# A hybrid attention block on one NeuronCore: seven-product keys and values in the stick-breaking units alone, the mask moved into the scan, the softmax scaling on VectorE, and the input's sums tied to their places

## The chip, the core and the metric

The kernel runs on one core of one Trainium2 chip. A core has a matrix engine (TensorE, in the profile PE, with its weight loads as PEld), a vector engine (VectorE, DVE), an engine for activation functions (ScalarE, ACT), a general engine (GpSimd, POOL) and a sync engine that issues DMAs (SyncE, SP). Each runs its own instructions in a fixed order; semaphores tie them together. Matrix results land in PSUM, everything else lives in SBUF. DMAs are issued from the queues of SP and ACT, and from GpSimd where the transfer has to add to what is already in its destination.

The metric is device time in microseconds of one execution, lower is better. The profiled execution is one execution out of several, and its trace lists each instruction with its start, its length and the source line that made it.

## The reference

One decoder block over 16 meta tokens and 512 tokens, 1024 wide, all in float32. Every token is normalized and projected to ten pieces. Eight heads do differential attention with ALiBi, sixteen heads of 64 do stick-breaking attention, both are gated with SiLU, projected, merged by sigmoid gates, projected once more and normalized over the residual. Cut to what matters here:

```python
proj = jnp.einsum('bld,dn->bln', h, w_in[i])
q_d, k_d, v_d, g_d, q_s, k_s, v_s, g_s, m_d, m_s = jnp.split(proj, IN_OFFSETS, axis=-1)

# differential attention, per head: two softmaxes, their difference weighs the values
s = einsum(q, k) * 64 ** -0.5 + alibi          # -inf where the key lies behind the query
p = softmax(s)
y_d = einsum(p[:, :, 0] - lam * p[:, :, 1], v)

# stick-breaking attention, per head; before: k_pos < q_pos
z = einsum(q, k) * 64 ** -0.5
log_keep = where(before, log_sigmoid(-z), 0)
suffix = cumsum_from_the_right(log_keep) - log_keep
a = where(before, exp(log_sigmoid(z) + suffix), 0)
y_s = einsum(a, v)

br_d = einsum(rms_norm(y_d) * (1 - lam_init) * silu(g_d), w_br_diff)
br_s = einsum(y_s * silu(g_s), w_br_sb)
y = einsum(sigmoid(m_d + b0) * br_d + sigmoid(m_s + b1) * br_s, w_out)
out = layer_norm(DN_ALPHA * h + y)
```

The queries come in five blocks: the 16 meta tokens, whose results are dropped, and four blocks of 128. A query block sees 144, 272, 400 or 528 keys.

## The kernel before

**Precision by three products.** [...] Each product of 128 x 128 weights with a piece of the input is three matmuls: high by high, high by low, low by high. A weight half (128 x 512) is loaded by SP (`fetch`, L134), rounded by ScalarE (`hi`, L160) and its remainder taken by VectorE (`lo`, L165). `prep` does this for one half, four halves ahead of use, and then lets `fetch` load what the rings of buffers have room for. `take` checks that the halves are used in the order of the list `seq`, from which `items` (what is split) and `loads` (what is loaded) are made ahead of time.

**Units.** The attention runs in 16 units: eight heads of differential attention (d0 to d7), then eight pairs of stick-breaking heads (s0 to s7). The loop at the end of the attention section runs, for unit u, a list of projections (keys and values of unit u + 1, the query of unit u + 2, and in the stick-breaking units two gate projections) and, woven into it at given points of a rough clock, the steps of unit u's own attention: scores, transposes, values. `run` walks the projections, adds up the time they are taken to need and drops each step in when its point has come.

**Keys and values by seven products.** `keys_values` picks one of two ways. In the plain way `stage_k` and `stage_v` (both through `proj_pos`, matmuls at L475) project each of the two 264-position halves of the input with all eight weight tiles: 2 x 2 x 8 x 3 = 96 matmuls of 264 columns. From unit number `SEVEN` on, `stage_kv` does it with seven block products in the manner of Strassen and Winograd: 7 x 4 x 3 = 84 matmuls (L626). That needs sums of weight blocks and of input blocks. Of the weights, with (a11, a12) and (a21, a22) for keys and values, the list has a21 - a11 and a21 + a22, made by a load of a21 and a second load that adds a11 or a22 to it (`accum_op=ALU.add` at L136, issued by GpSimd into the ring `rawk`), and two more sums that VectorE makes (`add`, L147). `stage_kv` also copies and combines its partial results (L637 to L646) on the way to the keys (L633) and to `vT`, the values before their transpose.

**The input's sums.** For the seven products the input halves are combined too: `input_sums(k)`, for k from 0 to 3, copies the meta columns (GpSimd, L597), makes four sums on VectorE (L599 to L602), rounds them on ScalarE (L604) and takes the remainder (L605). The results are `tS` and the list `tL`. The condition on u in the unit loop puts two of these calls into each of the two units ahead of the unit that first projects with them.

**Who orders the work.** In the start of the kernel and in everything behind the attention, `keep_order` ties each instruction to the one before it on its engine, as the program lists them. In the units there is no such tie, apart from a few that `behind` makes on ScalarE: there a planner simulates the program, as it is being built, and orders each engine's queue by when it thinks that the instructions can run. So the place in the program's text and the place in an engine's queue differ. `follow` adds a tie without a semaphore between two instructions.

**Differential attention** (`d_scores`). For each of four query blocks and two softmaxes: scores on PE (L692), bias and minimum on VectorE (L775), exponential with its sum on ScalarE (L779). Then VectorE takes reciprocals (L783), GpSimd scales the first softmax (L784, up to 128 x 528) and makes the small factor of the second (L785), and VectorE combines them into the weights (L786). The weights are transposed on PE (L698, L703), split (L708, L709) and multiplied with the values (`d_values`, to L803); squares and the norm follow (`d_norm`).

**Stick-breaking attention** (`s_scores`). Two sigmoids on ScalarE (L840 of minus z, L842 of z) give the shares kept and taken. GpSimd zeroes the taken shares in the diagonal block where the key is not before the query (L846). VectorE scans the kept shares from the right (L848): the state is multiplied by the kept share and then the greater of it and a mask `after` is taken; the mask is 1 where the key is not before the query, so that the state starts at 1 there. The product of taken share and scanned neighbour (L849) is the weight.

**Other names.** `ident` is the 128 x 128 identity. `L` is 528, `H2` 264, `P` 128, `NB` 4. `gate` multiplies a gate with an attention result on GpSimd (L491). `vT` has one buffer; so has each of the two tiles `e0`, `e1` for exponentials or sigmoids. `pj` is a ring of three PSUM banks for all projections.

Of the kernel before, what the change touches and what calls it, by code (L numbers as in the profile page):

```python
# [9 lines left out]
F32 = mybir.dt.float32  # L10
# [3 lines left out]
ALU = mybir.AluOpType  # L14
PSUM = bass.MemoryType.PSUM

P = 128
# [4 lines left out]
L = M + S  # L22
# [12 lines left out]

ORDERED = [mybir.EngineType.PE, mybir.EngineType.DVE, mybir.EngineType.Activation, mybir.EngineType.Pool]
WARM = 14
SEVEN = 4
TD = (0.85, 11.0, 14.5)
QOFF = [0, 96, 224, 352, 480]  # L40
LO, HI = slice(0, 64), slice(64, 128)
# [3 lines left out]
def hybrid_block_kernel(ctx: ExitStack, tc: tile.TileContext, x, meta, emb_g, emb_b, w_in, b_gate,  # L45
                        diff_lambda, subln_g, w_br_d, w_br_s, w_out, ln_g, ln_b, out):
    nc = tc.nc
    v, s, g, pe = nc.vector, nc.scalar, nc.gpsimd, nc.tensor
# [22 lines left out]
    for u, (kind, n) in enumerate(UNITS):  # L71
        if u + 1 < len(UNITS):
            other, i = UNITS[u + 1]
# [39 lines left out]
    for l in range(WOUT, len(loads)):  # L113
        left[l] = 1
    raw0 = ypool.tile([P, 4, KT, P], F32, tag="ys", name="raw0")
    raws, split, sums, later = {}, [], {}, []
    rings = {"raw": (6, []), "rawk": (4, []), "rawa": (4, [])}
    state = {"l": 0, "h": 0, "n": 0, "ahead": 4}
    pools = {"raw": wpool}
# [5 lines left out]
    def fetch(most=99):  # L125

        while state["l"] < len(loads) and most:
            l = state["l"]
            src, more, tag = loads[l]
            bufs, log = rings[tag]  # L130
            if len(log) >= bufs and left[log[-bufs]] or tag not in pools:
                return
            raw = pools[tag].tile([P, 4, P], F32, tag=tag, name=tag, bufs=bufs)
            nc.sync.dma_start(raw if l < WOUT else raw.rearrange("p a b -> p (a b)"), src)  # L134
            if more is not None:
                g.dma_start(raw, more, accum_op=ALU.add)  # L136
            raws[l] = raw
            log.append(l)
            state["l"] += 1
            most -= 1  # L140

    def add(h):

        first, second = items[h]
        one = sums.pop(True) if first is None else raws[first]
        raw = one if first is None else pools["sum"].tile([P, 4, P], F32, tag="sum", name="sum", bufs=1)
        v.tensor_tensor(raw, one, raws[second], op=ALU.add)  # L147
        for l in items[h]:
            if l is not None:
                left[l] -= 1  # L150
        sums[h] = sums[True] = raw

    def hi(h):

        assert len(split) == h
        item = items[h]
        raw = raw0[:, h // 2, ts(h % 2, 4)] if item is None else sums.pop(h) if isinstance(item, tuple) else raws[item]
        wh, wl = [wpool.tile([P, 4, P], F32R, tag=w, name=w, bufs=6) for w in ("wh", "wl")]
        split.append((raw, wh, wl))
        s.copy(wh, raw)  # L160
# [26 lines left out]
    def follow(ins, other):  # L187
        tc.add_manual_dep(ins, other.name, mybir.DependencyInfo(mybir.DependencyClass.NoSync, mybir.DependencyReason.DATA),
                          reason="order")

    def behind(name, on=True):

        if on:
            ins = nc.cur_bb.bb.instructions[-1]
            if name in state:
                follow(ins, state[name])
            state[name] = ins

    def keep_order(first, engines=ORDERED):

# [318 lines left out]
    with tc.tile_pool(name="att", bufs=1) as ap:  # L519
# [14 lines left out]
        for t in (v4d, v4s, *(tails[n][1] for n in tails)):  # L534
            g.memset(t.bitcast(F32), 0.0)
        E = [ap.tile([P, ZW], F32, name=f"e{c}") for c in range(2)]
        after, staged = [], []


        K = [ap.tile([P, 2, L], F32R, name=f"k{c}") for c in range(2)]  # L540
# [53 lines left out]
        def input_sums(k):  # L594


            g.tensor_copy(hP[k][:, :, :M], hM[:, k:k + 5:4])  # L597
            b11, b12, b21, b22 = [hP[k][:, m, ts(n, H2)] for m in range(2) for n in range(2)]
            v.tensor_tensor(b22, b12, b22, op=ALU.subtract)  # L599
            v.tensor_tensor(b12, b11, b12, op=ALU.subtract)  # L600
            v.tensor_tensor(b11, b22, b11, op=ALU.subtract)
            v.tensor_tensor(b21, b11, b21, op=ALU.add)  # L602
            h, l = tS[0][:, k:k + 5:4], pair_of("tl", F32R)
            s.copy(h, hP[k])  # L604
            v.tensor_tensor(l, hP[k], h.bitcast(F32), op=ALU.subtract)  # L605
            tL.append(l)
# [143 lines left out]
        def d_scores(unit, h):  # L750

            A = unit["A"]


            bias = ap.tile([P, L], F32, tag="bias", name="bias", bufs=2)
            if h == 0:
                g.iota(bias, pattern=[[-1, L]], base=400, channel_multiplier=1, allow_small_or_imprecise_dtypes=True)
                g.affine_select(bias, bias, pattern=[[-1, L]], compare_op=ALU.is_ge, fill=1e30, base=400,
                                channel_multiplier=1)
            g.tensor_scalar(bias, biases[-1] if h else bias, 0.5 if h else -0.5, None, op0=ALU.mult)  # L760
            biases.append(bias)
            a = apads[h % 2]
            mn = ap.tile([P, NB, 2, 2], F32, tag="mn", name="mn", bufs=2)
            zs = ap.tile([P, NB, 2], F32, tag="zs", name="zs", bufs=2)
            rz = ap.tile([P, NB, 2], F32, tag="rz", name="rz", bufs=2)
            for i in reversed(range(NB)):
                nk = NKEY[i]
                e = [E[c][:, ZOFF[i]:ZOFF[i] + nk] for c in range(2)]
                for c in range(2):
                    m = mn[:, i, c, :]  # L770
                    for n, (ps, k0, use) in enumerate(logits(A[c], K[c], i)):
                        if n == 1:
                            yield
# [9 lines left out]
                v.reciprocal(r, zs[:, i, :])  # L783
                g.tensor_scalar(e[0], e[0], r[:, 0:1], None, op0=ALU.mult)  # L784
                g.tensor_tensor(r[:, 1:2], r[:, 1:2], nlam, op=ALU.mult)  # L785
                v.scalar_tensor_tensor(a[:, AOFF[i]:AOFF[i] + nk], e[1], r[:, 1:2], e[0], op0=ALU.mult, op1=ALU.add)  # L786
                yield

# [41 lines left out]
        def s_scores(unit, c, first):  # L830
            A = unit["A"]
            a = apads[c]
            sg, om = E
            for i in reversed(range(NB)):
                nk, z0 = NKEY[i], ZOFF[i]
                for n, (ps, k0, use) in enumerate(logits(A[c], K[c], i)):
                    if n == 1:
                        yield
                    o = ds(z0 + k0, use)
                    s.activation(om[:, o], ps[:, :use], AF.Sigmoid, scale=-1.0)  # L840
                    behind("act", first)
                    s.activation(sg[:, o], ps[:, :use], AF.Sigmoid)  # L842
                    behind("act", first)

                own = sg[:, ds(z0 + nk - P, P)]
                g.affine_select(own, own, pattern=[[-1, P]], compare_op=ALU.is_gt, fill=0.0, base=0, channel_multiplier=1)  # L846
                rev = om[:, z0:z0 + nk][:, ::-1]
                v.tensor_tensor_scan(rev, rev, after[0][:, L - nk:][:, ::-1], 1.0, ALU.mult, ALU.max)  # L848
                v.tensor_tensor(a[:, ds(AOFF[i], nk - 1)], sg[:, ds(z0, nk - 1)], om[:, ds(z0 + 1, nk - 1)],  # L849
                                op=ALU.mult)  # L850
                yield
# [36 lines left out]
        for u, (kind, n) in enumerate(UNITS):  # L888
# [9 lines left out]
            if u + 4 in (SEVEN + 1, SEVEN + 2):  # L898
                if not tS:
                    tS.append(ypool.tile([P, KT, L], F32R, tag="ys", name="tS"))  # L900
                for m in range(2):
                    steps.append((5.0 + 6.0 * m, lambda k=2 * (u + 3 - SEVEN) + m: input_sums(k)))
            if kind == "d":
                ta = {}
                steps += spread(d_scores(unit, n), 0.0, TD[0], 10)
# [3 lines left out]
                pending = [(3.0 if n < 7 else 5.8, lambda unit=unit, n=n: d_norm(unit, n))]  # L909
            else:  # L910
                if n == 0:
                    after.append(ap.tile([P, L], F32, tag="bias", name="after", bufs=2))
                    g.memset(after[0], 0.0)
                    own = after[0][:, L - P:]
                    g.affine_select(own, own, pattern=[[-1, P]], compare_op=ALU.is_gt, fill=1.0, base=0, channel_multiplier=1)
                    for a in apads:
                        for i in range(NB):
                            g.memset(a[:, ds(AOFF[i] + NKEY[i] - 1, 1)], 0.0)
# [259 lines left out]
```

## Time and profile before

| what | value |
|---|---|
| median of three runs | 742.61 us |
| lowest and highest of the three | 742.55 and 744.74 us |
| the profiled execution's own time | 746.39 us |
| its span, from the first to the last instruction | 744.7 us |
| mean granted clock of TensorE | 0.983 |
| DMA over the span | 105.02 MB, 141 GB/s |
| GpSimd's DMA queue | 12.06 MB, 12.8% of 16 engines' span |

How to read it: the page gives for each engine its busy time, then groups of instructions with count, busy time, mean length and the idle time just ahead of them with the instruction that ended it. Matmuls are pipelined and each is drawn longer than the distance to the next one, so a busy PE does not by itself mean that nothing can be gained; the distance from start to start tells what a matmul takes, and PE's waits and the granted clock tell what is lost. The chain of waits follows the work that ended last back through whoever released it. An engine's idle time counts only where this chain runs through it.

The units can be told apart in the trace by the query projections, each of which ends with ScalarE rounding the query (L551): between two of these lie one unit's projections. The start lies ahead of 37 us, the units with differential heads reach to about 250 us, the stick-breaking ones to about 545 us, and the projections behind them to the end.

### The profile page before, as it was taken

To read this page: it belongs to the slowest core of one execution; us is meant where nothing else is said; L and a number is where in the kernel's file an instruction comes from. 1 tells how busy PE (TensorE), PEld (TensorE's weight loads), DVE (VectorE), ACT (ScalarE), POOL (GpSimd) and SP (SyncE) were. 2 spreads that over 40 slices of the span, in tenths; PEclk is the share of its full clock that TensorE was granted. 3 is DMA by queue.
4 is the path that set the end of the run, shared out by engine and by line. 5 is a ranking of instruction groups with operands and counts; after the bars stand their busy time and mean duration, and the time that the engine had idled before them with its cause. 6 is when DMAs were issued, how large, how long until landed. Compare 5 with 4: busy or idle time off the path is not lost.

```text
span 744.7 us, 13453 instructions
## 1 busy us (share of the span) xinstructions
PE 716.7 (96%) x4546; PEld 651.2 (87%) x4546; DVE 597.4 (80%) x1214; ACT 441.2 (59%) x1043; POOL 212.3 (29%) x269
## 2 busy tenths in 40 slices
PE   8899999998999898999999999999999999999995
PEld 8799999987988787888989898988888998899885
DVE  6986678887888767979797989878566778688897
ACT  5675667676667966656656565656544555656300
POOL 3343453453463313232323121214002201240002
PEclk9989999999999998999999999999999999999998
DMA  9374444647555544455655524395229747787802
GB/s 291 89 153 119 133 98 114 162 104 164 141 113 130 136 128 108 135 123 144 140 158 117 140 90 126 104 304 147 71 83 184 157 100 180 147 169 186 320 27 105
DMA packets 160135, 105.02 MB, mean 141 GB/s; under 512 B 7441, under 2 KB 148146, under 8 KB 160066
## 3 DMA queue, kind: packets, MB, share of 16 engines
q1 hardware_dynamic: 137762, 91.04, 41.5%
q0 software_dynamic: 21984, 12.06, 12.8%
q10 hardware_dynamic: 320, 1.06, 0.4%
q8 instruction: 36, 0.59, 0.3%
q14 instruction: 33, 0.27, 0.1%
HBM read 82.53 MB, written 7.86 MB: 121 GB/s over the span
## 4 chain that ended last, share of the span: by engine, by line
PE 80%; DVE 7%; DMA 4%; POOL 3%; issue 3%; ACT 3%; SPq 0%; ACTq 0%; DVEq 0%; POOLq 0%
PE q L626 15%; PE ps L460 11%; PE ps L459 11%; PE ps L461 11%; PE q L985 9%; PE ps L475 6%; PE sc L692 5%; PE t L698 3%; DMA lgb<-in_ln_b_dram 1%; PE t L703 1%; DMA rawk<-in_w_in_dram 1%; PE bank L350 1%; PE av L862 1%; PE av L863 1%; POOL e L784 1%
## 5 line engine op out<-in xcount | busy, mean ns | idle before, releaser
L165 DVE TENSOR_TENSOR wl<-raw,wh 128x512 fp32r<-128x512 f32 x168 | 121.2, 726 | 41.7 <-ACT wh L160 40.2
L460 PE MATMUL ps<-hTl,wh 128*128 128x512 f32 x368 | 146.7, 399 | 0.0
L459 PE MATMUL ps<-hTh,wh 128*128 128x512 f32 x368 | 145.8, 396 | 0.0
L461 PE MATMUL ps<-hTh,wl 128*128 128x512 f32 x368 | 145.3, 395 | 0.0
L160 ACT CAST wh<-raw 128x512 fp32r<-128x512 f32 x168 | 102.9, 621 | 35.5 <-PE ps L460 20.6
L461 PEld LDWEIGHTS ps<-hTh,wl 128*128 128x128 f32 x368 | 69.6, 189 | 12.9
L459 PEld LDWEIGHTS ps<-hTh,wh 128*128 128x128 f32 x368 | 69.6, 189 | 12.8
L460 PEld LDWEIGHTS ps<-hTl,wh 128*128 128x128 f32 x368 | 69.6, 189 | 12.1
L692 PE MATMUL sc<-k,A 128*128 128x264 f32 (+3 forms) x320 | 66.7, 301 | 4.1 <-ACT e L842 2.3
L846 POOL TENSOR_SCALAR_AFFINE_SELECT e<-e 128x128 f32<-128x128 f32 x64 | 43.6, 702 | 93.0 <-ACT e L842 84.5
L985 PE MATMUL q<-gh,wl 128*128 128x256 f32 x224 | 63.9, 285 | 0.0
L985 PE MATMUL q<-gl,wh 128*128 128x256 f32 x224 | 63.7, 284 | 0.0
L985 PE MATMUL q<-gh,wh 128*128 128x256 f32 x224 | 63.2, 282 | 0.2 <-ACT t L994 0.2
L784 POOL TENSOR_SCALAR e<-e,rz 128x528 f32<-128x528 f32 (+3 forms) x32 | 46.1, 1441 | 56.9 <-DVE rz L783 56.9
L136 POOL DMA_DIRECT2D rawk<-in_w_in_dram x24 | 32.4, 1381 | 99.5 <-DMA rawk<-in_w_in_dram 62.2
L709 DVE TENSOR_TENSOR al<-t,ah 128x512 fp32r<-128x512 f32 (+2 forms) x88 | 45.7, 525 | 18.4 <-ACT ah L708 11.2
L692 PEld LDWEIGHTS sc<-k,A 128*128 128x128 f32 x320 | 51.4, 192 | 9.2 <-ACT e L842 2.7
L848 DVE TENSOR_TENSOR_SCAN e<-e,after 128x528 f32<-128x528 f32 (+1 forms) x64 | 55.4, 871 | 4.8 <-ACT e L840 4.6
L708 ACT CAST ah<-t 128x512 fp32r<-128x512 f32 (+2 forms) x88 | 40.1, 464 | 30.0 <-PE t L698 21.9
L626 PE MATMUL q<-tS,wh 128*128 128x264 f32 x192 | 56.0, 292 | 0.8 <-DVE A L552 0.7
L626 PE MATMUL q<-tl,wh 128*128 128x264 f32 x192 | 55.4, 289 | 0.0
L626 PE MATMUL q<-tS,wl 128*128 128x264 f32 x192 | 55.0, 288 | 0.0
(278 smaller groups left out, 1976.7 us busy)
## 6 DMA issues: line engine op xcount, KB each, us to landing
raw<-in_w_in_dram SPq DMA_DIRECT2D x140, 256.0 KB, 3.1
k<-ks SPq DMA_DIRECT2D x60, 132.0 KB, 2.7
rawk<-in_w_in_dram SPq DMA_DIRECT2D x24, 256.0 KB, 3.4
rawk<-in_w_in_dram POOLq DMA_DIRECT2D x24, 256.0 KB, 5.2
raw<-in_w_out_dram SPq DMA_DIRECT2D x16, 256.0 KB, 3.7
k<-ks SPq DMA_DIRECT2D x60, 66.0 KB, 2.2
raw<-in_w_br_diff_dram SPq DMA_DIRECT2D x12, 256.0 KB, 3.4
raw<-in_w_br_sb_dram SPq DMA_DIRECT2D x12, 256.0 KB, 4.2
```

Source lines behind the costliest of these rows:

```text
L160: s.copy(wh, raw)
L165: eng.tensor_tensor(wl, raw, wh.bitcast(F32), op=ALU.subtract)
L459: pe.matmul(ps, wh[:, k % 4, :], hTh[:, k, M:], start=(k == 0), stop=False)
L460: pe.matmul(ps, wh[:, k % 4, :], hTl[:, k, M:], start=False, stop=False)
L461: pe.matmul(ps, wl[:, k % 4, :], hTh[:, k, M:], start=False, stop=(k == KT - 1))
L475: pe.matmul(ps[:, :H2], a[:, k % 4, :], b[:, k, ts(c, H2)], start=(k == 0 and m == 0), stop=(k == KT - 1 and m == 2))
L626: pe.matmul(bank, a[:, k, :], b, start=start and k == 0 and j == 0, stop=k == 3 and j == 2, skip_group_check=not start)
L692: pe.matmul(ps[:, :n], q, K[:, m, k0:k0 + n], start=(m == 0), stop=(m == 1))
L709: v.tensor_tensor(l, t[:, o:o + w], h.bitcast(F32), op=ALU.subtract)
L784: g.tensor_scalar(e[0], e[0], r[:, 0:1], None, op0=ALU.mult)
L848: v.tensor_tensor_scan(rev, rev, after[0][:, L - nk:][:, ::-1], 1.0, ALU.mult, ALU.max)
L985: pe.matmul(bank, a[:, k, :], b[:, n, k, :], start=start and k == 0 and m == 0, stop=k == 3 and m == 2, skip_group_check=not start)
```

## The change

1. `SEVEN` goes from 4 to 8: the units d4 to d7 project keys and values in the plain way, and the seven products begin with s0. The conditions on `SEVEN` follow: the input's sums are now called in the units d5 and d6, and `seq`, `items` and `loads` have plain weight halves for d4 to d7.
2. The accumulating second load is no longer issued in `fetch` right behind the first. It is kept in `second` and issued by `added`: for the ring `rawk` two calls of `prep` later, or at once where an `add` or a `hi` needs it before; for the ring `rawa`, used behind the attention, at once as before.
3. A new helper `placed` runs a piece of the program and ties its first instruction on each named engine behind the last one that the program lists there. The accumulating loads are placed on GpSimd, the input's sums on all four engines.
4. In `d_scores` the scaling and the small factor move from GpSimd to VectorE.
5. In `s_scores` the mask on GpSimd goes. The scan starts from 0 in place of 1, and its second operand is the identity in the last 128 columns: the state is 0 until the query's own key, 1 there, and the running product of kept shares behind it. A weight multiplies a taken share with the scanned neighbour, which is now 0 wherever the key is not before the query.

```diff
-SEVEN = 4
+SEVEN = 8
...
             nc.sync.dma_start(raw if l < WOUT else raw.rearrange("p a b -> p (a b)"), src)
             if more is not None:
-                g.dma_start(raw, more, accum_op=ALU.add)
+                second[l] = lambda raw=raw, more=more: g.dma_start(raw, more, accum_op=ALU.add)
+                later.append((state["n"] + (2 if tag == "rawk" else 0), lambda l=l: added(l)))
+                later.sort(key=lambda x: x[0])
+                if tag == "rawa":
+                    added(l)
...
+    def added(l):
+
+        if l in second:
+            placed(second.pop(l), ORDERED[3:])
+
     def add(h):
 
-        first, second = items[h]
+        first, other = items[h]
+        for l in items[h]:
+            added(l)
...
     def hi(h):
...
         item = items[h]
+        added(item)
...
+    def placed(work, engines=ORDERED):
+
+        ins = nc.cur_bb.bb.instructions
+        n = len(ins)
+        work()
+        for e in engines:
+            new = next((i for i in ins[n:] if i.engine == e), None)
+            old = next((ins[m] for m in range(n - 1, max(n - 400, 0), -1) if ins[m].engine == e), None)
+            if new is not None and old is not None:
+                follow(new, old)
...
                 v.reciprocal(r, zs[:, i, :])
-                g.tensor_scalar(e[0], e[0], r[:, 0:1], None, op0=ALU.mult)
-                g.tensor_tensor(r[:, 1:2], r[:, 1:2], nlam, op=ALU.mult)
+                v.tensor_scalar(r[:, 1:2], r[:, 1:2], nlam, None, op0=ALU.mult)
+                v.tensor_scalar(e[0], e[0], r[:, 0:1], None, op0=ALU.mult)
...
-                own = sg[:, ds(z0 + nk - P, P)]
-                g.affine_select(own, own, pattern=[[-1, P]], compare_op=ALU.is_gt, fill=0.0, base=0, channel_multiplier=1)
                 rev = om[:, z0:z0 + nk][:, ::-1]
-                v.tensor_tensor_scan(rev, rev, after[0][:, L - nk:][:, ::-1], 1.0, ALU.mult, ALU.max)
+                v.tensor_tensor_scan(rev, rev, diag[0][:, L - nk:][:, ::-1], 0.0, ALU.mult, ALU.max)
...
-                    steps.append((5.0 + 6.0 * m, lambda k=2 * (u + 3 - SEVEN) + m: input_sums(k)))
+                    steps.append((5.0 + 6.0 * m, lambda k=2 * (u + 3 - SEVEN) + m: placed(lambda: input_sums(k))))
...
-                    after.append(ap.tile([P, L], F32, tag="bias", name="after", bufs=2))
-                    g.memset(after[0], 0.0)
-                    own = after[0][:, L - P:]
-                    g.affine_select(own, own, pattern=[[-1, P]], compare_op=ALU.is_gt, fill=1.0, base=0, channel_multiplier=1)
+                    diag.append(ap.tile([P, L], F32, tag="bias", name="diag", bufs=2))
+                    g.memset(diag[0], 0.0)
+                    g.tensor_copy(diag[0][:, L - P:], ident)
```

More of the change, by code (lines that the diff above doesn't have):

```diff
@@ L115, in hybrid_block_kernel @@
     raw0 = ypool.tile([P, 4, KT, P], F32, tag="ys", name="raw0")
-    raws, split, sums, later = {}, [], {}, []
+    raws, second, split, sums, later = {}, {}, [], {}, []
     rings = {"raw": (6, []), "rawk": (4, []), "rawa": (4, [])}
@@ L140, in fetch @@
             most -= 1
+    def added(l):
+        if l in second:
+            placed(second.pop(l), ORDERED[3:])
     def add(h):
-        first, second = items[h]
+        first, other = items[h]
+        for l in items[h]:
+            added(l)
         one = sums.pop(True) if first is None else raws[first]
         raw = one if first is None else pools["sum"].tile([P, 4, P], F32, tag="sum", name="sum", bufs=1)
-        v.tensor_tensor(raw, one, raws[second], op=ALU.add)
+        v.tensor_tensor(raw, one, raws[other], op=ALU.add)
         for l in items[h]:
@@ L536, in hybrid_block_kernel @@
         E = [ap.tile([P, ZW], F32, name=f"e{c}") for c in range(2)]
-        after, staged = [], []
+        diag, staged = [], []
         K = [ap.tile([P, 2, L], F32R, name=f"k{c}") for c in range(2)]
```

## The prediction

> **What bounds the kernel now.** I read the page first.
>
> ```profile
> span 744.7 us, 13453 instructions
> PE 716.7 (96%) x4546; PEld 651.2 (87%) x4546; DVE 597.4 (80%) x1214; ACT 441.2 (59%) x1043; POOL 212.3 (29%) x269
> PE 80%; DVE 7%; DMA 4%; POOL 3%; issue 3%; ACT 3%; SPq 0%; ACTq 0%; DVEq 0%; POOLq 0%
> ```
>
> TensorE (PE) carries 80% of the chain that ends last, so time can leave only where PE waits, or runs at a lower clock after a wait. Next I read the waits of PE alone: who waited for whom, us in total, times, longest. These are the ones over 0.5 us behind the first matmuls.
>
> ```profile
> PE q L626 <- DVE vT L646: 6.1, 4, 2.4
> PE av L863 <- DVE al L709: 3.6, 1, 3.6
> PE ps L475 <- ACT k L569: 2.5, 1, 2.5
> PE sc L692 <- ACT e L842: 2.3, 1, 2.3
> PE sc L692 <- POOL k L542: 1.2, 1, 1.2
> PE q L626 <- DVE A L552: 0.7, 1, 0.7
> ```
>
> Then PE by stretches, cut where the clock changes: the stretch, its length, PE's busy time and count, the granted clock, DMA share and GB/s.
>
> ```profile
> 36.46:43.29 6.83, 6.14 (x28) 0.50 1.11 144
> 186.65:190.06 3.41, 3.41 (x18) 0.50 0.09 20
> 254.91:258.33 3.42, 3.42 (x11) 0.50 0.00 0
> 285.63:292.46 6.83, 5.17 (x21) 0.50 0.56 115
> ```
>
> The four longest waits each meet a stretch at half clock, which costs about half its length again: 3.4, 1.7, 1.7 and 3.4 us. In four groups by place: **G1**, the start: 2.5 + 1.2 + 3.4 = 7.1. **G2**, the units d3 to d7, waits for the values' copy vT and for A: 6.1 + 0.7 + 1.7 = 8.5. **G3**, at 253 us, where the scores' PSUM waits for ScalarE: 2.3 + 1.7 = 4.0. **G4**, at 287 us in the first stick-breaking unit s0: 3.6 + 3.4 = 7.0. Together 26.6.
>
> The chain of waits in three of these places shows who is late (start, us, what).
>
> ```profile
> 31.52 0.04 POOLq L525
> 33.40 0.53 POOL k L542
> 35.75 0.90 ACT tS L604
> 36.73 0.38 ACT k L569
> 37.15 1.03 PE ps L475 x3
> ...
> 173.33 4.67 DMA rawk<-in_w_in_dram
> 178.56 1.28 POOL rawk L136
> 179.84 1.66 POOL e L784
> 185.49 0.44 DVE vT L646
> 185.97 1.14 PE q L626 x6
> ...
> 284.82 0.83 POOL e L846
> 287.29 0.50 PE av L863
> ```
>
> First block: the input sums' ScalarE cast (L604), written in units d1 and d2, runs in the start between PE and the first keys. Second: GpSimd's queue sits on the accumulating load, so the softmax scaling behind it (L784) is late, then the copy of the values, then PE. Third: the same in s0 with the mask (L846). In G2 and G4, then, attention is late by a queue, not by a full engine.
>
> **The change part by part.**
>
> **Seven products for four units fewer.** d4 to d7 go from 84 to 96 matmuls of 264 columns.
>
> ```profile
> 440.75 2.70 PE q L626 x22
> L165 DVE TENSOR_TENSOR wl<-raw,wh 128x512 fp32r<-128x512 f32 x168 | 121.2, 726 | 41.7 <-ACT wh L160 40.2
> L599 DVE TENSOR_TENSOR hF<-hF x4: 425/428/430, 29.9 to 31.7; 128x264 f32<-128x264 f32 x4
> 66.40:90.80 24.40, 24.40 (x175) 23.12 (x174) 17.14 (x48) 15.99 (x43) 8.53 (x10) 1.00 0.41 109
> 159.20:183.40 24.20, 23.24 (x161) 21.44 (x159) 19.62 (x50) 15.12 (x39) 10.40 (x11) 1.00 0.71 159
> 183.40:209.80 26.40, 24.00 (x157) 22.56 (x157) 21.27 (x55) 18.15 (x48) 12.05 (x13) 0.94 0.57 131
> 209.80:234.10 24.30, 22.62 (x159) 21.06 (x157) 21.22 (x53) 17.62 (x48) 11.06 (x17) 1.00 0.51 127
> ```
>
> A dense run spaces them 2.70/22 = 0.123 us, so 4 x 12 x 0.123 = **+5.9** on PE, with nothing to hide it. The last four rows are one unit each, cut where a query projection is rounded (busy time and count of PE, PEld, DVE, ACT, POOL, then the clock). The first, with plain products, takes 24.4 us with PE busy throughout. Those with seven have 12 x 0.123 = 1.5 us less for PE, 22.9, and still take 24.2, 26.4 and 24.3. Plain products hardly lengthen these units, because the waits of G2 fill the difference. VectorE loses three splits and two sums per unit, 5 x 0.726, and three half-width evictions of 0.43 (the 264 columns of L599): 4.9 us. ScalarE loses three casts. Twelve loads of 256 KB go, eight of them accumulating, and with these the queue's block in most of G2.
>
> **The scaling from GpSimd to VectorE.** Per head four multiplies and four small products change engine.
>
> ```profile
> L784 POOL TENSOR_SCALAR e<-e,rz 128x528 f32<-128x528 f32 (+3 forms) x32 | 46.1, 1441 | 56.9 <-DVE rz L783 56.9
> L303 DVE TENSOR_SCALAR xn<-xt,xmv,xrs 128x512 f32<-128x512 f32 x7 | 3.5, 532 | 1.7 <-POOL xrs L265 1.7
> 31.23 0.21 DVE L413 TENSOR_SCALAR nlam<-lexp 128x1 f32<-128x1 f32 x1
> DVE apad L786 <- POOL rz L785: 9.4, 10, 2.4
> ```
>
> The nearest row is L303, 532 ns for 512 columns. A head has 528 + 400 + 272 + 144 = 1344, so 1.4 us, and 4 x 0.21 = 0.8 for the small ones: 2.2 of VectorE per head. The upper end is 2.7, at the 726 ns of L165; the lower is below nothing, because VectorE's own waits for GpSimd, 9.4/8 = 1.2 per head, go. I take 2.2, as load. It lies beside PE while VectorE has room: the plain unit's 17.1 of 24.4 becomes 19.3. In the chain of a head a step of 1.4 us on GpSimd becomes one of about 0.4, without a crossing of engines. On the sum this is worth nothing by itself, since PE sets the unit.
>
> **The scan without the mask.** 64 selects leave GpSimd. The scan keeps its size and count (only its start value and second operand differ). The new diagonal, a memset and one copy, I cost at nothing; GpSimd is 29% busy, and without that cover it would be one instruction.
>
> ```profile
> L846 POOL TENSOR_SCALAR_AFFINE_SELECT e<-e 128x128 f32<-128x128 f32 x64 | 43.6, 702 | 93.0 <-ACT e L842 84.5 <-DMA ydT<-gd 2.9 <-DVE apad L849 2.8
> POOL rawk L136 <- DMA rawk<-in_w_in_dram: 62.2, 9, 10.9
> ```
>
> **The accumulating loads put off.** GpSimd waited 62.2 us for the first half of such a tile. Issued two splits later, it finds more of them landed. Behind it in GpSimd's queue then stand the gate products, the bias and the rest of the square, and none of these is in PE's waits above. The sum on VectorE that reads the tile could come late: 0, or one landing as at 173 us, +4.7. I take 0, because loads are fetched several tiles ahead. With the mask gone this is the cure of G4: **-5.0** of 7.0, bounds 0 and -7.0, with 2.0 left for lag that d7 hands on.
>
> **The input sums to their places**, now d5 and d6.
>
> ```profile
> L605 DVE TENSOR_TENSOR tl<-hF,tS x4: 1240/1254/1495, 37.2 to 43.6; 128x1056 fp32r<-128x1056 f32 x4
> 35.70 0.43 DVE L568 TENSOR_TENSOR k<-ps,k 64x264 fp32r<-64x264 f32 x1
> ```
>
> They ran from 30 to 44 us. By L599's row the first two start ahead of nlam (L413), which ends at 31.44; the att buffers lie in the memory that the start gives back then, and GpSimd goes on at 31.52. More of them stand ahead of the key remainder L568, whose chain with ScalarE's L569 releases PE at 37.15. PE's 48 products were done 1.2 us before the memset's end at 33.9, near 32.8. Without the sums nlam ends 0.7 earlier, the memset too, and the key evictions (four to six steps of about 0.4) end near 33.3. G1 shrinks to about 0.5 us. A gap that short should cost no clock: three of the four vT waits, 6.1 - 2.4 = 3.7 together, had no half clock behind them. So **-6.6**, bounds 0 and -7.1.
>
> In d5 and d6 they add 16 x 0.425 + 4 x 1.254 = 11.8 to VectorE, 5.9 a unit: 17.1 + 2.2 + 5.9 = 25.2 against PE's 24.4. This is the weak point. I expect a lag of a few us that PE covers with projections, and a piece of G2 to stay: **-6.0** of 8.5. Bounds: -8.5, and +9.6 (rival A, which takes G3 and G4 with it).
>
> **G3** I leave, **0** (bounds -4.0 and 0): its release is ScalarE's own, at the change from the exponential to the sigmoid, which no edit moves.
>
> On the clock, the trace has a half-speed stretch behind a wait of 2.4 us (186 us). [...]
>
> **Sum.** +5.9 - 6.6 - 6.0 - 5.0 = -11.7. The profiled execution took 746.39 (span 744.7 and 1.7 around it), so another like it would take 734.7. The median of the three runs is 742.61, 3.8 lower, and I forecast that: **730.9**.
>
> **The rivals.**
>
> A, the one that ends slower: VectorE becomes the bound in d5, d6 and d7. For it: 25.2 us of work in 24.4. Price: from 159 to 210 us, where attention lagged, VectorE was busy 40.89 of 50.6 us, a share of 0.81. At that share d5 and d6 take 25.2/0.81 = 31.1, 6.7 over each, and d7 takes (21.2 + 2.2)/0.81 = 28.9 against 22.9 of PE, 6.0 over: 19.4 of waits. The waits of G2 to G4, 12.7, had 6.8 of clock behind them, so about half as much again: 29.1 in place of 19.5. That gives 742.6 + 5.9 - 6.6 + 9.6 = **751.5**. It decides from the point where waits and clock behind 115 us pass 20.2. Against it: the share of 0.81 came with VectorE's waits for GpSimd and with GpSimd's for loads, which leave. 0.13, of it 0.03 where it stops within 0.3% of before.
>
> B, the tie does not do what it says: only the first instruction of each engine is tied, or other early work takes the sums' place. G1 stays: **737.5**. Against it: the later sums read what the first wrote. 0.13.
>
> C, lag from d5 to d7 lands in s0, and G4 stays: **735.9**. For it: the last step there, al L709, is VectorE's own. 0.13.
>
> D, no wait is left at all, G3's too, if PE has projections in hand there: 742.6 + 5.9 - 26.6 = **721.9**. Against it: nothing takes ScalarE's change of function away. 0.13.
>
> **How the numbers follow.** The forecast has 0.48, with 726 to 735 for itself. D reaches down to 721.9, B and C up to 737.5, and the milder part of A to about 740. The range is 721 to 740 and leaves out most of A. About 0.3% (2.2 us) is what a measurement of this kernel can tell from no change. Faster: 0.48 + 3 x 0.13 = 0.87, less 0.02 for B and C together with some of A, 0.85; within 0.3% 0.05; slower 0.10.
>
> **What would show it.** Right: L599 to L605 run in d5 and d6; PE's gap near 33 us is under 1 us, with full clock up to 60 us; d3 to d6 without the sums take some 24.4 us with PE full; GpSimd has no L784 or L846; PE's waits and clock behind 115 us come to 9 or less. VectorE busy over 24 us of a unit in d5 and d6, with PE waiting behind it, shows A. The forecast is wrong where PE waits for tS, tl or vT at d7, where the start's wait stays over 2 us, or where another step of VectorE ends PE's wait in s0.

## The result, and the profile after

| | before | after |
|---|---|---|
| median | 743.67 us (4 runs, 742.55 to 746.83) | 732.33 us (4 runs, 731.37 to 734.11) |
| ratio of the two | | 0.9843, 95% interval 0.9805 to 0.9882 |
| span of the profiled execution | 744.7 us | 732.3 us |
| mean granted clock | 0.983 | 0.993 |

The changed kernel is 11.3 us faster by the medians and 12.4 by the spans; 730.9 was forecast, in a range of 721 to 740. In the listing of the changed kernel the lines are some 23 higher: L626 is now L649, L692 L715, L784 L808, L848 L869. First the page after.

```profile
span 732.3 us, 13316 instructions
PE 713.7 (97%) x4594; PEld 649.9 (89%) x4594; DVE 585.8 (80%) x1246; ACT 428.9 (59%) x1023; POOL 111.9 (15%) x133
```

PE has 48 matmuls more (4594 for 4546), as the four plain units ask, and the span is shorter all the same. GpSimd's busy time is nearly halved. The waits of PE after, those over 0.4 us behind the first matmuls of the kernel and ahead of the last projection:

```profile
PE av L880 <- DVE a L752: 3.0, 1, 3.0
PE t L726 <- DVE al L732: 1.3, 1, 1.3
PE q L649 <- DVE vT L669: 0.5, 1, 0.5
```

All of G1 to G4 is gone from this list. The start first, in the chain of waits after:

```profile
32.72 0.54 POOL k L565
33.31 0.39 PE sc L715
```

PE goes on at 33.3 in place of 34.1 and 37.2, and no half clock follows (1.00 from 33 to 60 us). Then the units (stretch, length, and busy time and count of PE, PEld, DVE, ACT, POOL, then clock, DMA share, GB/s): one plain unit without input sums and the two with them.

```profile
134.10:157.50 23.40, 23.40 (x167) 22.13 (x166) 17.07 (x54) 15.03 (x42) 5.80 (x6) 1.00 0.50 109
157.50:182.70 25.20, 25.20 (x183) 23.92 (x182) 22.65 (x66) 17.88 (x46) 3.39 (x2) 1.00 0.60 143
182.70:207.40 24.70, 24.70 (x178) 23.35 (x177) 23.50 (x67) 18.27 (x45) 3.04 (x3) 1.00 0.34 90
```

PE is busy in every one of them, also where VectorE is busy 23.50 of 24.70 us, 95%. G3 was the change of ScalarE from exponentials to sigmoids. The groups of its table loads, before and then after, without the one at the very start:

```profile
L840 ACT ACT_TABLE_LOAD x3 | 3.8, 1283 | 0.1
L779 ACT ACT_TABLE_LOAD x1 | 1.3, 1283 | 0.0
L821 ACT ACT_TABLE_LOAD x1 | 1.3, 1283 | 0.0
L823 ACT ACT_TABLE_LOAD x1 | 1.3, 1283 | 0.0
L819 ACT ACT_TABLE_LOAD x1 | 1.3, 1283 | 0.0
```

```profile
L863 ACT ACT_TABLE_LOAD x2 | 2.6, 1283 | 0.0
L842 ACT ACT_TABLE_LOAD x1 | 1.3, 1283 | 0.0
```

Before, s0's first sigmoids (L840) stood in ScalarE's queue ahead of d6's norm (L821, L823) and d7's last softmax (L779), so the tables went back and forth: seven loads of 1.28 us, 9.0 in all. L819 (L842 after) is the load ahead of d7's own norm, which falls among s0's sigmoids in both kernels. After there are three loads. So G3 too was attention being late: d6 and d7 were not done when s0 began.

What is new is the wait of 3.0 us near 336 us. The timeline of GpSimd and of VectorE there (start, length; in brackets the idle time before), and then the stretch behind it with its clock:

```profile
323.00 1.30 POOL L514 TENSOR_TENSOR ys<-sg,ys 128x512 f32<-128x512 f32 x1 [11.74 <-DVE ys L888]
324.24 2.60 POOL L136 DMA_DIRECT2D rawk<-in_w_in_dram  x2
334.14 0.69 DVE L158 TENSOR_TENSOR sum<-rawk,raw 128x512 f32<-128x512 f32 x1 [5.12 <-DMA rawk<-in_w_in_dram]
```

```profile
336.33:339.74 3.41, 3.33 (x11) 0.50 0.47 138
```

The two accumulating loads stand on GpSimd behind a gate product that waited 11.74 us for VectorE. They are issued at 324 us, and VectorE's sum (L158) stands still for 5.12 us until they land; behind it in VectorE's queue waits what PE needs. PE runs 3.41 us at 0.50 here. The wait of 1.3 us near 440 us has the same chain:

```profile
429.88 7.91 DMA rawk<-in_w_in_dram
437.82 0.69 DVE sum L158
439.41 0.59 DVE al L732
440.05 0.33 PE t L726
```

### The profile page after: what moved, and what is told of

Same layout as the page of the kernel before. It is cut to its first block, busy times and chain, and to the rows that moved or that the text cites. A ratio compares the mean times of both kernels' runs of the same rounds, so it can differ in the third digit from the quotient of the medians.

```text
span 732.3 us, 13316 instructions
## 1 busy us (share of the span) xinstructions
PE 713.7 (97%) x4594; PEld 649.9 (89%) x4594; DVE 585.8 (80%) x1246; ACT 428.9 (59%) x1023; POOL 111.9 (15%) x133
## 4 chain that ended last, share of the span: by engine, by line
PE 64%; issue 16%; DMA 7%; DVE 7%; POOL 4%; ACT 3%; SPq 0%; POOLq 0%; DVEq 0%; ACTq 0%
PE ps L498 12%; PE ps L484 9%; PE ps L482 9%; PE ps L483 9%; PE q L1005 8%; PE q L649 4%; PE sc L715 4%; PE t L721 2%; DMA raw<-in_w_out_dram 2%; DMA ss<-sm 1%; POOL rawk L136 1%; PE bank L373 1%; DMA rawk<-in_w_in_dram 1%; PE t L726 1%; POOL yd L514 1%
## 5 line engine op out<-in xcount | busy, mean ns | idle before, releaser
L177 DVE TENSOR_TENSOR wl<-raw,wh 128x512 fp32r<-128x512 f32 x172 | 119.2, 698 | 43.1 <-ACT wh L172 42.6
L172 ACT CAST wh<-raw 128x512 fp32r<-128x512 f32 x172 | 105.4, 622 | 40.2 <-PE ps L483 28.9
L484 PEld LDWEIGHTS ps<-hTh,wl 128*128 128x128 f32 x368 | 69.5, 189 | 13.3
L482 PEld LDWEIGHTS ps<-hTh,wh 128*128 128x128 f32 x368 | 69.5, 189 | 13.2 <-DVE kvt L666 0.5
L483 PEld LDWEIGHTS ps<-hTl,wh 128*128 128x128 f32 x368 | 69.4, 189 | 12.6
L498 PE MATMUL ps<-hTh,wh 128*128 128x264 f32 x256 | 73.6, 288 | 0.0
L498 PE MATMUL ps<-hTl,wh 128*128 128x264 f32 x256 | 73.4, 287 | 0.0
L498 PE MATMUL ps<-hTh,wl 128*128 128x264 f32 x256 | 73.3, 287 | 0.0
L715 PE MATMUL sc<-k,A 128*128 128x264 f32 (+3 forms) x320 | 66.2, 297 | 0.2 <-POOL k L565 0.2
L869 DVE TENSOR_TENSOR_SCAN e<-e,diag 128x528 f32<-128x528 f32 (+1 forms) x64 | 55.6, 876 | 3.7 <-ACT e L863 3.3
L715 PEld LDWEIGHTS sc<-k,A 128*128 128x128 f32 x320 | 50.4, 189 | 3.5 <-POOL k L565 0.4
L498 PEld LDWEIGHTS ps<-hTh,wl 128*128 128x128 f32 x256 | 48.3, 189 | 0.5
L498 PEld LDWEIGHTS ps<-hTl,wh 128*128 128x128 f32 x256 | 48.3, 189 | 0.4
L498 PEld LDWEIGHTS ps<-hTh,wh 128*128 128x128 f32 x256 | 48.3, 189 | 0.4
```

The costliest lines, as they stand in the source:

```text
L177: eng.tensor_tensor(wl, raw, wh.bitcast(F32), op=ALU.subtract)
L482: pe.matmul(ps, wh[:, k % 4, :], hTh[:, k, M:], start=(k == 0), stop=False)
L483: pe.matmul(ps, wh[:, k % 4, :], hTl[:, k, M:], start=False, stop=False)
L484: pe.matmul(ps, wl[:, k % 4, :], hTh[:, k, M:], start=False, stop=(k == KT - 1))
L498: pe.matmul(ps[:, :H2], a[:, k % 4, :], b[:, k, ts(c, H2)], start=(k == 0 and m == 0), stop=(k == KT - 1 and m == 2))
L715: pe.matmul(ps[:, :n], q, K[:, m, k0:k0 + n], start=(m == 0), stop=(m == 1))
```

## The experiments

Each kernel is compared with runs of the kernel before on the same chip, whose medians were 745.4, 744.7, 746.0 and 745.5 us in the four groups, so the ratios compare better across groups than the times.

| kernel | median, us | ratio to before (95%) | span, us |
|---|---|---|---|
| the change | 732.33 | 0.9843 (0.9805 to 0.9882) | 732.3 |
| a1, loads early, untied | 729.08 | 0.9781 (0.9755 to 0.9808) | 727.5 |
| a2, SEVEN = 4 | 739.22 | 0.9910 (0.9877 to 0.9942) | 737.4 |
| b1, before + sums tied | 740.05 | 0.9928 (0.9906 to 0.9950) | 741.2 |
| a3, scaling on GpSimd | 740.00 | 0.9918 (0.9893 to 0.9943) | 740.1 |
| a7, a1 + SEVEN = 4 | 732.97 | 0.9849 (0.9830 to 0.9867) | 731.3 |
| a8, a1 + scaling on GpSimd | 730.21 | 0.9813 (0.9797 to 0.9830) | 727.7 |
| a9, a1 + mask on GpSimd | 732.10 | 0.9838 (0.9810 to 0.9865) | 730.8 |
| a5, a1 + sums untied | 731.55 | 0.9831 (0.9813 to 0.9849) | 729.4 |
| a6, loads late, untied | 732.54 | 0.9814 (0.9765 to 0.9863) | 730.7 |
| b2, before + SEVEN = 8 | 732.33 | 0.9815 (0.9790 to 0.9840) | 730.7 |
| c1, a1 + SEVEN = 7 | 731.96 | 0.9811 (0.9782 to 0.9840) | 731.0 |
| b4, b2 + sums tied | 730.52 | 0.9808 (0.9782 to 0.9833) | 727.7 |

### a1: the accumulating loads early and untied

```diff
-                later.append((state["n"] + (2 if tag == "rawk" else 0), lambda l=l: added(l)))
-                later.sort(key=lambda x: x[0])
-                if tag == "rawa":
-                    added(l)
+                second.pop(l)()
```

> The changed kernel, but each accumulating load is issued right behind its first half and untied, as before the change. Theory 1: the new waits of PE in the stick-breaking units (3.0 us and its half clock 1.7 near 336 us, 1.3 us near 440 us) come from tying the accumulating load behind the gate product on GpSimd, so that VectorE's sum and ScalarE's rounding wait for its landing. Then these waits go, VectorE's 9.9 us of waits for rawk fall under 2, and the time is 726.5 (724 to 729). Rival: lag from d5 and d6 is the cause; then they stay in some place and the time is 731 to 733. A second rival: the early accumulating loads block GpSimd as before the change and PE waits in s0 return, 735 or more.

Theory 1 held. The span is 727.5, 4.8 under the change's. VectorE's waits for rawk are down from 9.9 us to 0.4, and the longest wait of PE behind 60 us is this one, with no half clock until the end of the kernel (mean 0.996):

```profile
PE q L646 <- DVE tl L625: 0.6, 1, 0.6
```

### a2: seven products in the differential units after all

```diff
-SEVEN = 8
+SEVEN = 4
```

> The changed kernel with SEVEN = 4: d4 to d7 have seven products again, the sums of the input are tied into d1 and d2. Theory 1 (the waits of G2 came from GpSimd's queue): with scaling and mask off GpSimd PE does not wait in d3 to d7, PE's work falls by 5.9 us, and the time is 726 to 728, less what tied accumulating loads cost. Theory 2 (VectorE's own load makes attention late there, 21.2 + 2.2 = 23.4 us a unit against 22.9 of PE): waits for vT stay, 5 us or more with their clock between 130 and 260 us, and the time is 732 to 740.

739.22, in theory 2's range: PE has less to do and the kernel is 5.1 us longer by the span. PE waits near 160 us for VectorE, with 3.40 us at a clock of 0.50 behind it, and then often and shortly up to 250 us, though hardly for vT (0.5), which theory 2 had named; ScalarE loads tables seven times at the change to s0. But accumulating loads were tied here too, so a7 separates the two.

```profile
PE q L649 <- DVE ks L656: 2.6, 2, 2.4
PE sc L715 <- DMA k<-ks: 1.2, 1, 1.2
```

### b1: the input's sums tied, alone

```diff
-                    steps.append((5.0 + 6.0 * m, lambda k=2 * (u + 3 - SEVEN) + m: input_sums(k)))
+                    steps.append((5.0 + 6.0 * m, lambda k=2 * (u + 3 - SEVEN) + m: placed(lambda: input_sums(k))))
```

> The kernel before with one part of the change: the input's sums tied to their places in d1 and d2. Theory: the start's wait and its half clock go (7.1 us by the profile of before), and 11.8 us of VectorE work in d1 and d2 is covered: 743.7 - 6.9 = 736.8 (735 to 739). Rival: VectorE is late in d1 and d2 for it and the waits of G2 begin earlier and grow: 740 to 744.

740.05: the rival's number. The start's wait is gone as in the change, but VectorE is busy 53.74 of 59 us in d1 and d2 (44.97 in the kernel before), and PE's waits begin earlier; the stretch, then PE's waits:

```profile
66.00:125.00 59.00, 58.03 (x402) 53.88 (x400) 53.74 (x142) 43.80 (x112) 26.95 (x29) 1.00 0.42 108
```

```profile
PE sc L703 <- DVE rz L794: 2.1, 1, 2.1
PE q L637 <- DVE vT L657: 1.4, 1, 1.4
```

### a3: the scaling back on GpSimd

```diff
-                v.tensor_scalar(r[:, 1:2], r[:, 1:2], nlam, None, op0=ALU.mult)
-                v.tensor_scalar(e[0], e[0], r[:, 0:1], None, op0=ALU.mult)
+                g.tensor_scalar(e[0], e[0], r[:, 0:1], None, op0=ALU.mult)
+                g.tensor_tensor(r[:, 1:2], r[:, 1:2], nlam, op=ALU.mult)
```

> The changed kernel with the softmax scaling and its small factor back on GpSimd. Theory 1 (it was the accumulating load ahead of the scaling in GpSimd's queue that made attention late): in d3 to d6 no such load is left, so PE waits there stay under 1 us in all and the time is 731 to 734. Theory 2 (the crossing to GpSimd and its 1.4 us by itself makes attention late): waits of 3 us or more in d4 to d7, table loads of ScalarE doubled at the change to s0, 736 to 742.

740.0, the number of theory 2, but not for its reason, and it loaded no more tables. The chain ahead of its longest wait (5.8 us) runs through a tied accumulating load that stands behind the scaling:

```profile
210.85 9.29 DMA rawk<-in_w_in_dram
220.16 0.07 DVE sum L158
222.91 0.82 PE sc L715 x2
```

### a7: a1 with SEVEN = 4

> a1 (the changed kernel with its accumulating loads early and untied) with SEVEN = 4. Theory 2 of a2 (VectorE's own load makes attention late where seven products and the scaling share a unit): waits of PE and clock between 130 and 260 us of 6 us or more, seven or more table loads of ScalarE, 735 to 740. Rival: the waits of a2 came from tied accumulating loads alone; then PE does not wait there and 5.9 us less of PE work give 723 to 725.

733.0, 2 us under the range of theory 2, and by most of its signs: the loads are not in the way any more, and still PE waits 7.4 us in all between 120 and 260 us, with 6.8 us at half clock, and ScalarE loads tables six times at the change, where seven or more were expected. That is more than the 5.9 us of PE's work that it saves. The largest of PE's waits, then a stretch of 60 us:

```profile
PE sc L712 <- DVE mn L795: 4.2, 3, 2.4
```

```profile
120.00:180.00 60.00, 56.19 (x372) 51.01 (x370) 54.53 (x147) 40.83 (x108) 12.40 (x9) 1.00 0.61 142
```

VectorE is busy 54.53 of 60 us here, and 57.22 in the 60 us before, which hold the input's sums of d1 and d2. The lag seems to begin there, and units with 22.9 us of PE work leave VectorE little room to make it up.

### a8: a1 with the scaling on GpSimd

> a1 with the softmax scaling and its small factor back on GpSimd. In a3 two things were mixed: scaling on GpSimd, and tied accumulating loads behind the scaling, for whose landing VectorE's sum waited 3.9 us. Theory 1: without the tie the scaling on GpSimd costs little in plain units, PE waits under 2 us in d3 to d7: 728 to 731. Theory 2: the crossing by itself makes attention late: 734 to 740.

730.2 and a span of 727.7, beside 727.5: theory 1. Without tied loads behind it the scaling does little harm in plain units. PE waits 2.1 us for the input's sums at the start of d7, where a1 has a wait of 0.6 for them:

```profile
PE q L646 <- DVE tl L625: 1.1, 1, 1.1
PE q L646 <- ACT tS L624: 1.0, 1, 1.0
```

### a9: a1 with the mask on GpSimd

```diff
+                own = sg[:, ds(z0 + nk - P, P)]
+                g.affine_select(own, own, pattern=[[-1, P]], compare_op=ALU.is_gt, fill=0.0, base=0, channel_multiplier=1)
                 rev = om[:, z0:z0 + nk][:, ::-1]
```

> a1 with the mask of the stick-breaking weights back on GpSimd (a select on the diagonal block; the scan stays as changed, so the select is idle work for the result). Theory (G4 came from the mask behind an accumulating load in GpSimd's queue): PE waits of 2 to 5 us with clock come back in s0 or s1, 731 to 736. Rival (G4 came from lag that the differential units hand on): no wait of over 1 us, the same time as a1 within 1.5 us.

732.1, 3.3 us over a1 by the span, as the theory had it. The chain shows the mask (L866) behind the landing of an accumulating load, and the row after it the half clock behind PE's wait of 2.8 us:

```profile
265.09 5.35 DMA rawk<-in_w_in_dram
271.79 0.84 POOL e L866
274.23 0.32 DVE apad L869
274.69 0.63 PE t L718 x4
```

```profile
275.40:278.80 3.40, 3.40 (x18) 0.51 0.00 0
```

### a5: a1 with the input's sums untied

> a1 with the input's sums untied. The planner draws them into the start again, as before the change. Theory: the start's wait and its half clock come back (+7) and VectorE in d5 and d6 is relieved of 11.8 us, which gives nothing as PE does not wait there: 735 to 737. Rival: the sums in d5 and d6 cost something that PE's waits do not show; then 732 to 734.

731.55, a miss of both. The start's waits of 1.2 and 2.5 us are back to the tenth, and the first query that L571 rounds comes at 66.1 us in place of a1's 59.8; yet the span is only 1.9 us over a1's. The half clock behind the waits is 3.4 us long where the kernel before had 6.83, and a1's wait of 0.6 for the sums at d7 goes. The longer wait of the start, then the half clock:

```profile
PE ps L495 <- ACT k L589: 2.5, 1, 2.5
```

```profile
36.70:40.10 3.40, 2.90 (x13) 0.50 0.92 125
```

### a6: the loads late, but untied

```diff
-            placed(second.pop(l), ORDERED[3:])
+            second.pop(l)()
```

> The changed kernel with its accumulating loads still called two splits later, but not tied behind the instruction that the program lists before them on GpSimd. It separates the delay from the tie. If the tie does the harm (the load stands behind a gate product that waits for VectorE): waits of PE over 1 us behind 300 us are gone and the time is that of a1, 727.5 to 730 beside a before of 744.7. If the delay does it (two splits are less than a landing): waits for rawk on VectorE stay over 5 us and the time stays near 732.

By the waits the tie does the harm: VectorE waits only 0.4 us for rawk, and PE has no wait of over 1 us behind 300 us. The time did not follow, though: 732.54, with an interval too wide to tell it from the change or from a1. The planner put s0's first sigmoids ahead of d6's norm here, ScalarE loads tables six times at the change, and PE waits there, the longest being

```profile
PE av L817 <- DVE yd L849: 1.1, 1, 1.1
```

### b2: the kernel before with SEVEN = 8 alone

> The kernel before with SEVEN = 8 alone; scaling, mask and loads as before, sums untied. Theory: plain units free VectorE and GpSimd in d3 to d6 together, so PE's waits between 60 and 230 us (8.5 with clock, G2) go and ScalarE's table loads at the change to s0 fall from seven to three (G3, 4.0); G1 stays and so do waits in s0 (G4, mask behind accumulating loads): 744.7 + 5.9 - 8.5 - 4.0 = 738 (735 to 740). Rival: GpSimd's scaling keeps attention late by itself: table loads six or more, 742 to 747.

732.3, against 738 expected, with scaling, mask, loads and sums as before. The one constant gives as much as the whole change. G2 and G3 are gone, as expected, with three table loads; G1 stays, with a half clock of 3.4; and G4, expected to stay, is down to one wait of 1.3 us without half clock (1.00 from 140 to 300 us). Two of PE's waits, then the stretch from d6 into s0 at full clock:

```profile
PE ps L475 <- ACT k L569: 2.5, 1, 2.5
PE av L859 <- DVE a L729: 1.3, 1, 1.3
```

```profile
180.00:240.00 60.00, 60.00 (x418) 56.33 (x418) 46.00 (x118) 42.60 (x106) 22.09 (x33) 1.00 0.52 125
```

### c1: a1 with SEVEN = 7

> a1 with SEVEN = 7: d7 has seven products, the input's sums stand in d4 and d5. PE's work falls by 1.5 us. If one unit of 23.4 us of VectorE work against 22.9 can be covered: 727.5 beside a1's 729 (a before of 744.7). If it makes attention late at the change to s0: PE waits of 2 us or more between 220 and 270 us and more than three table loads, 730 to 734.

731.96: no gain. PE waits 2.4 us near 202 us, where d7 begins, earlier than expected, with 3.4 us at half clock behind it, and ScalarE has three table loads and no more. The wait is for the transfer of d7's keys. Their first half is made by 194.3 us (L653), but SP issues it only from 201.5 on (second row), as d6's last scores, which read the same key tiles, end; so attention is late at d7.

```profile
PE sc L712 <- DMA k<-ks: 2.4, 1, 2.4
201.50 0.47 SPq L601 DMA_DIRECT2D k<-ks  x1
```

### b4: SEVEN = 8 and the sums tied, nothing else

> The kernel before with two parts of the change: SEVEN = 8 and the input's sums tied into d5 and d6. Against a1 it lacks the scaling on VectorE and the scan without the mask. If these two parts are worth something once the units are plain: waits of PE in s0 of 3 us with clock (as in a9) and in d6 of 2 us (as in a8), ratio to before 0.982 to 0.987. If they are worth nothing measurable: no wait of over 1.5 us behind 60 us, ratio 0.977 to 0.980, the same as a1's 0.9781. The start's wait of 3.7 us with its clock, which b2 has, is gone in both cases.

The ratio is 0.9808, between the two expectations, and its interval overlaps those of a1 and a9. The span is 727.7 beside a1's 727.5. The waits of a8 at d7 are there, with 3.40 us at a clock of 0.50 behind them; that of a9 in s0 is not, though the mask is on GpSimd here too, so the mask alone does not make it. With plain units and the sums in place the moves of scaling and mask are together worth nothing that these runs can tell from zero.

## Why the prediction came out

The time and the sign were right, and the plain products and G1 were sized within 0.3 us. That the sum came out is in part luck: G3 and the accumulating loads were wrong by 4.0 and 6.0 us, G2 and G4 were 2.5 and 2.0 too small, 1.9 us at the end lay in no term, and these errors nearly cancelled.

**Plain products, +5.9.** Right: 48 matmuls more, and the units d1 to d6 take 23.3 to 25.5 us with PE full.

**G1, -6.6.** In the trace 6.9: a wait of 0.2 is left and no half clock. As a part of the new kernel it is worth 6.3 us at the first query, but only 1.9 of span (a5). Of the 4.4 between, 0.6 is a1's wait for the sums where they now stand, and 1.7 lies in the end of the kernel, which took a1 55.8 us and a5 54.1 and which no edit touches (more on it below). The rest was not traced.

**G2, -6.0.** All 8.5 went. I kept a piece for VectorE's lag in d5 and d6, and rival A hung on it; VectorE did come to 23.50 of 24.70 us, and PE did not wait. A plain unit gives attention 24.4 us of PE work to hide behind, and the units ahead of d5 bring no lag along. My reading that attention was late "by a queue, not by a full engine" was half of it at most: a7 takes the queue away and keeps the seven products, and attention is late there behind a VectorE that is busy 91% of the time. How the 8.5 us divide between queue and VectorE in the kernel before stays open; seven products there with untied sums and nothing of attention on GpSimd was not tried.

**G3, 0.** Wrong. The step that failed is "its release is ScalarE's own, at the change from the exponential to the sigmoid, which no edit moves". The change of tables is ScalarE's, but that it happened seven times and not three came from d6 and d7 being late, and b2, where only the constant changes, has three loads and no wait there. The runs a1, a8 and b4 have three as well, and a2, a7 and b1, whose differential units are late, six or seven. The number is no measure of lateness by itself, since the planner orders ScalarE's queue: a6 has six with plain units, a3 and c1 have three with waits of 5.8 and 2.4 us at d7. -4.0 in place of 0, rival D's term.

**G4, -5.0.** The wait in s0 went (7.0). The mechanism, the mask behind a landing, is what a9 shows; but b2 has the same mask and loads and only 1.3 us, so a part of G4 was lag from the differential units as well. That is rival C's mechanism, which C expected to stay in the changed kernel and which went with it.

**The accumulating loads, 0.** Wrong: 3.0 + 1.7 of clock + 1.3 = 6.0 us lost. I named a late sum on VectorE, with 4.7 as its bound, and took 0 because loads are fetched several tiles ahead. What failed is that step: it looked at the delay of two splits and left out the tie. The load tied behind a gate product went out only after that product's own wait, 11.74 us in the row above. a1 gives back 4.8.

**What no step had.** From the last seven-product projection to the end the span is 1.9 us longer, which is the time between the last start in these rows and the end of the span, 53.5 before and 55.4 after. The groups of the last such projection, before and then after:

```profile
L985 PE MATMUL q<-gh,wh x224: 279/282/388, 577.8 to 691.2; 128*128 128x256 f32 x112
```

```profile
L1005 PE MATMUL q<-gh,wh x224: 279/281/387, 563.1 to 676.9; 128*128 128x256 f32 x112
```

No line of the change runs there, and PE waits for loads in both. In the fourteen traces this stretch takes from 53.2 to 56.5 us without following any edit, so the 1.9 is scatter as far as they show; its cause was not looked for. The account: 5.9 - 6.9 - 8.5 - 4.0 - 7.0 + 6.0 = -14.5 up to the first projection in these rows, where the trace has 577.8 and 563.1, -14.7. With the 1.9 it is -12.6, and the spans differ by -12.4.

**The scaling's price, 2.2 per head.** Near: VectorE's four multiplies take 484, 424, 353 and 291 ns, 1.55 us, and the four small ones 0.85, 2.4 together. VectorE's own combination (L786, L809 after) got cheaper in the mean, at 400 columns 632 ns after and 979 before, but not because the scaling left GpSimd. Of those eight before six took 631 to 635 ns, and the two long ones, 2383 and 1643 ns, ran beside the remainder of the square, which stays on GpSimd. The longer one:

```profile
105.41 2.38 DVE L786 SCALAR_TENSOR_TENSOR apad<-e,rz,e 128x400 f32<-128x400 f32 x1
105.53 1.82 POOL L809 TENSOR_TENSOR sql<-sq,sqh 128x512 fp32r<-128x512 f32 x1
```

Another of the six, at 129 us, overlapped the same GpSimd instruction (1.61 us) and took 635 ns, so why the two were long is not shown.

## What to carry to other kernels

Fewer operations on the bounding engine can cost time where they load the engine that feeds it (a7 has 5.9 us less of PE's work than a1 and a span 3.8 us longer): what counts is each stage's work on both engines, side by side, and the lag that a stage hands on, which can show up far behind as someone else's wait. A transfer tied behind an instruction is as late as that one: here two went out behind a gate product that had waited 11.74 us, and without the ties and the delay the span was 4.8 us shorter. So a transfer's issue belongs ahead of instructions that wait for other engines. Undo the parts of a bundle one by one and together: here one constant carried the gain, one part cost 5 us, and two were together worth nothing measurable, though undoing one of them, the mask, alone cost 3.3.

## What the runs showed of the hardware

In these runs the half clock behind a wait came in stretches of about 3.41 us or twice that (6.83), and neither its coming nor its length followed from the length of the wait alone. The same two waits of 1.2 and 2.5 us in the start were followed by 6.83 us in the kernel before and by 3.4 in a5 and b2. Two waits of 1.0 and 1.1 us brought one stretch in b4, and the same two in a8 brought none.

What differs is where the waits fall. In the kernel before the full-speed stretches between half ones (43.29 to 186.65, 190.06 to 254.91 and 258.33 to 285.63 us) last 143.36, 64.85 and 27.30 us, which is 42, 19 and 8 times 3.413: each change of the clock there lies a whole number of steps of 3.413 us behind the one before. In b4 both waits lie within one such step, and PE is busy for 1.69 us of it; in a8 they lie in two steps, and PE is busy 2.32 and 2.28. The step of b4 and the one behind it, then the two of a8:

```profile
210.98:214.40 3.42, 1.69 (x6) 1.00 0.48 158
214.40:217.80 3.40, 2.90 (x12) 0.50 0.65 81
```

```profile
209.83:213.25 3.42, 2.32 (x14) 1.00 0.45 149
213.25:216.66 3.41, 2.28 (x15) 1.00 0.87 144
```

The kernels before and after, cut in such steps from their own changes of the clock up to 700 us, are like these two: at full clock, the steps with PE busy for 0.48, 1.02, 1.20 and 1.52 us (before) and 0.53 us (after) were followed by half clock, and those with 1.73 us or more (before) and 2.14 us or more (after) were not. Half clock went on for another step where PE was busy 2.72 and 1.76 us in the first one (before); it ended behind steps with 3.41 and 3.42 us (before), 3.33 (after) and, in a5 and b4, 2.90. This is read from the traces; no run was made to test it.
